# Low parts of the input projection's weights: from one GpSimd subtraction per block to two VectorE pieces

## The chip, the cores and the metric

The kernel runs on one core of one Trainium2 chip, as one program. The metric is device time in microseconds (us), the median of three runs. Engines are named as in the profile: PE is TensorE (PEld its weight loads), DVE is VectorE, ACT is ScalarE, POOL is GpSimd, SP is the engine from whose queue most DMAs are issued.

## What is computed

One decoder layer over 1024 tokens of width 1024, in float32: a combined input projection that feeds a sparse attention branch (NSA) and an RWKV-7 branch, their merge, a cross-attention, and a grouped mixture of experts. What matters here is the first step and its two users:

```python
z_nsa, z_rwkv, z_gate = split(x @ w_in)          # x: 1024 tokens by 1024
o_nsa  = nsa_attention(...)                      # reads z_nsa
o_rwkv = rwkv7_time_mix(...)                     # reads z_rwkv; a scan over the tokens
y = (sigmoid(..) * (o_nsa @ p_nsa) + sigmoid(..) * (o_rwkv @ p_rwkv)) @ w_out
```

The operands of the projection's matmuls are split in two: a high part (the value rounded to fp32r) and a low part (the value minus its high part). A product is then three matmuls: high by high, low by high, high by low.

## The kernel before, in words

The input projection goes by blocks of 128 output columns, 41 in all (40 of 128 columns and one of 24). For each block `weights` loads 512 KB of w_in into the tile `wraw` (one buffer, line 114, on SP's queue), rounds it into `wh` on ACT (line 117, one instruction of 128x1024) and subtracts to get `wl` on POOL (line 118, one instruction of 128x1024). `wh` and `wl` have two buffers each, so the weights of one block are made while the block before is multiplied. `halves` then runs, for each half of the tokens, 8 groups of three matmuls (lines 35 to 37: `xh,wh`, `xl,wh` and `xh,wl`; only the third reads `wl`) into one of two PSUM banks, and an evacuation on ACT or DVE or both: lines 220 to 227 for RWKV blocks, 184/185, 198/199 and 209 for attention blocks, 238 for the 16 gate blocks. The evacuated tile `ev` (three buffers) is stored to memory.

The first two blocks (12 and 13 of the RWKV columns) are made while x itself is loaded, transposed on PE (line 74) and split by ACT and DVE (line 28).

Beside the blocks run 8 items of the RWKV branch (`Rwkv.steps`). Each item forms its factors on ACT, DVE and POOL, inverts triangular matrices by rows on DVE (lines 850 and 851: 31 pairs of short instructions between SBUF tiles, `xinv` and `tinv`), applies the inverses on PE (line 869, evacuated at 872, 875, 877 and 880), and then runs a chain of 8 sequential steps on PE and ACT (lines 902, 904, 908, 909). The end of an item (lines 916 to 938) normalises its output. After the last item the RWKV buffers are given to the attention, whose loads and compression (`Nsa.__init__`, `compress`, lines 335 to 390) run beside the last gate blocks; then the attention proper begins on PE at lines 465 and 467.

The order of the blocks and items in the program is a string written out by hand (`ORDER`). The order of instructions on each engine's queue is not: the framework's context (`schedule_with_timeline_sim=True` in `kernel`) lays every queue out before the run, by its own estimate of when each instruction could begin. So projection matmuls stand between the small matmuls of the RWKV items one by one. On the chip each queue runs strictly in the order laid out: an instruction that has to wait holds up all that stand behind it on its engine.

Of the kernel before, what the change touches and what calls it, by code (L numbers as in the profile page):

```python
# [7 lines left out]
F32 = mybir.dt.float32  # L8
# [3 lines left out]
ALU = mybir.AluOpType  # L12
# [69 lines left out]
class Inproj:  # L82
# [28 lines left out]
    def weights(self, c0, w, p0=None):  # L111
        nc, pw = self.k.nc, self.pw
        raw = (p0.tile([128, 8, 128], F32, tag="wraw0", bufs=2, name="wraw0") if p0 else pw.tile([128, 8, 128], F32, tag="wraw", bufs=1, name="wraw"))[:, :, :w]
        nc.sync.dma_start(raw, self.w_in[:, :, c0:c0 + w])
        wh = pw.tile([128, 8, 128], F32R, tag="wh", bufs=2, name="wh")[:, :, :w]
        wl = pw.tile([128, 8, 128], F32R, tag="wl", bufs=2, name="wl")[:, :, :w]
        nc.scalar.copy(wh, raw)  # L117
        nc.gpsimd.tensor_tensor(wl, raw, wh.bitcast(F32), ALU.subtract)  # L118
        return wh, wl

    def ev(self, dt=F32):
# [91 lines left out]
    def r_block(self, b, weights=None, tag=None):  # L213
        nc, s = self.k.nc, self.k.s
        st = {}

        def evac(acc, ns):
            t, o = self.ev(), self.ev()
            m, m1 = self.mu[:, b:b + 1], self.mu1[:, b:b + 1]
            nc.scalar.mul(t, acc, m)  # L220
            nc.vector.scalar_tensor_tensor(o[:, 1:], acc[:, 1:], m1, t[:, :511], ALU.mult, ALU.add)
            if ns.start == 0:
                nc.vector.tensor_scalar(o[:, :1], acc[:, :1], m1, None, ALU.mult)
                st["c"] = self.pw.tile([128, 1], F32, tag="rc", bufs=2, name="rc")
                nc.gpsimd.tensor_scalar(st["c"], t[:, 511:512], 1.0, 1.0, ALU.mult, ALU.mult)
            else:
                nc.vector.scalar_tensor_tensor(o[:, :1], acc[:, :1], m1, st["c"], ALU.mult, ALU.add)
            nc.sync.dma_start(s["r", b][:, ns], o)
        if weights:
            return self.halves(*weights, evac, tag)  # L230
        self.block(1304 + 128 * b, evac)
# [162 lines left out]
class Nsa:  # L394
# [47 lines left out]
    def attention(self):  # L442
# [6 lines left out]
        with tc.tile_pool(name="nq", reuse_waits="tile", bufs=1) as self.pq, tc.tile_pool(name="nw", reuse_waits="tile", bufs=2) as pw, tc.tile_pool(name="np", reuse_waits="tile", bufs=2, space=PSUM) as ps:  # L449
            def front(br, g, qt, t, st):  # L450
# [6 lines left out]
                for i in range(4):  # L457
# [18 lines left out]
                    st[br, i] = pt  # L476
                    yield
                w = weights(g, qt, sums, slice(bi + 1, bi + 2))
                for i in range(4):
                    nc.gpsimd.tensor_scalar(st[br, i][:, :n], st[br, i][:, :n], w[:, 0, i:i + 1], 1.0, ALU.mult, ALU.mult)  # L480
# [11 lines left out]
            def compressed(g, qt, t, st):  # L492

                qs = slice(128 * qt, 128 * qt + 128)
                sums = pw.tile([128, 1, 4], F32, tag="csum", name="csum")
                sc = ps.tile([128, 512], F32, tag="pt", bufs=PTB, name="sc")
                for i in range(4):
                    o = sc[:, 64 * i:64 * i + 64]
                    nc.tensor.matmul(o, t["q"][:, i, qs], kch[:, g, :], start=True, stop=False)
                    nc.tensor.matmul(o, t["q"][:, i, qs], kcl[:, g, :], start=False, stop=True)  # L500
                pc = pw.tile([128, 4, 64], F32, tag="pc", name="pc")
                mc = pw.tile([128, 4], F32, tag="mc", name="mc")
                nc.vector.tensor_tensor(pc, sc[:, :256].rearrange("p (h n) -> p h n", h=4),
                                        tcm[:, 4 * g:4 * g + 4, 56 - 8 * qt:120 - 8 * qt], ALU.add)
                nc.vector.tensor_reduce(mc, pc, AX.X, ALU.max)
                nc.vector.tensor_scalar(mc, mc, -1e29, None, ALU.max)
                nc.gpsimd.tensor_tensor(pc, pc, mc.unsqueeze(2).to_broadcast([128, 4, 64]), ALU.subtract)
                nc.scalar.activation(pc, pc, AF.Exp)
                nc.vector.tensor_reduce(sums[:, 0], pc, AX.X, ALU.add)
                w = weights(g, qt, sums, slice(0, 1))  # L510
                nc.gpsimd.tensor_tensor(pc, pc, w[:, 0, :].unsqueeze(2).to_broadcast([128, 4, 64]), ALU.mult)
                st["c"] = pc
# [1405 lines left out]
```

## Time and profile before

| what | value |
| --- | --- |
| median of 3 runs | 1859.53 us (1857.18 to 1862.02) |
| the profiled execution's own time | 1859.28 us |
| its span on the core | 1857.5 us |
| mean granted TensorE clock | 0.961 of full |

The span is what the trace covers; the time of an execution has 1.8 us more around it. Rows of the trace give a start and a duration in us from the span's start; in a timeline row a bracket at the end gives how long the engine stood idle before the instruction and what released it.

### The profile page before, as it was taken

What the parts mean: (1) busy time and instruction counts of PE and PEld (TensorE: products, weight loads), DVE (VectorE), ACT (ScalarE), POOL (GpSimd) and SP (SyncE); (2) the same over time, 40 slices, a digit from 0 to 9 for tenths busy, and PEclk for the clock granted to TensorE, in tenths of its full rate; (3) what the DMA queues carried; (4) which work ended last, traced back from release to release, by engine and by line L of the source; (5) the groups of instructions that cost most, each with busy time, mean ns of one, the idle gap of its engine ahead of it and who ended that gap; (6) DMA issues with size and microseconds to landing.
All of it is one profiled execution on the core that took longest, in us unless ns stands there. A gap on an engine that the chain in (4) does not pass through costs nothing. (4 is left out here: it accounts for less than half of the span.)

```text
span 1857.5 us, 27257 instructions
## 1 busy us (share of the span) xinstructions
PE 1740.5 (94%) x9254; PEld 1419.5 (76%) x9254; DVE 1203.8 (65%) x2738; ACT 845.1 (45%) x1756; POOL 534.5 (29%) x681
## 2 busy tenths in 40 slices
PE   8999989999999999999998899999997999999992
PEld 6877767787678878888886678877796888888871
DVE  3225757768775202599886675556986777777786
ACT  4223313344333221398886441034304676676672
POOL 1123202222122211266566121100024333333214
PEclk9999979999999999999999899999978999999996
DMA  7354335344523228702102764033324999999974
GB/s 230 117 177 119 114 112 166 114 139 128 147 84 89 93 81 245 239 10 83 41 10 64 245 196 161 23 99 125 135 93 149 317 294 296 294 300 303 310 278 151
DMA packets 252797, 295.95 MB, mean 159 GB/s; under 512 B 63789, under 2 KB 150981, under 8 KB 252144
## 3 DMA queue, kind: packets, MB, share of 16 engines
q1 hardware_dynamic: 245184, 273.52, 45.1%
q0 software_dynamic: 7472, 20.67, 4.6%
q8 instruction: 74, 1.21, 0.3%
q14 instruction: 67, 0.55, 0.1%
HBM read 231.88 MB, written 70.98 MB: 163 GB/s over the span
## 5 line engine op out<-in xcount | busy, mean ns | idle before, releaser
L35 PE MATMUL acc<-xh,wh 128*128 128x512 f32 (+1 forms) x656 | 268.1, 409 | 8.4 <-ACT wh L117 3.3
L36 PE MATMUL acc<-xl,wh 128*128 128x512 f32 (+1 forms) x656 | 268.6, 410 | 0.0
L37 PE MATMUL acc<-xh,wl 128*128 128x512 f32 (+1 forms) x656 | 266.6, 407 | 0.2 <-POOL wl L118 0.2
L1529 DVE TENSOR_TENSOR wlo<-wraw,whi 128x512 fp32r<-128x512 f32 x384 | 237.6, 684 | 32.3 <-ACT whi L1528 32.0
L1528 ACT CAST whi<-wraw 128x512 fp32r<-128x512 f32 x384 | 206.1, 621 | 19.3 <-issue 17.8
L118 POOL TENSOR_TENSOR wl<-wraw,wh 128x1024 fp32r<-128x1024 f32 (+1 forms) x41 | 99.0, 2414 | 295.0 <-ACT wh L117 284.5
L35 PEld LDWEIGHTS acc<-xh,wh 128*128 128x128 f32 (+1 forms) x656 | 124.2, 189 | 44.1 <-ACT wh L117 4.2
L37 PEld LDWEIGHTS acc<-xh,wl 128*128 128x128 f32 (+1 forms) x656 | 123.9, 189 | 36.0 <-issue 8.1
L36 PEld LDWEIGHTS acc<-xl,wh 128*128 128x128 f32 (+1 forms) x656 | 124.4, 190 | 33.9 <-issue 6.6
L475 ACT ACTIVATE pp<-pp,nm 128x640 f32<-128x640 f32 (+7 forms) x128 | 94.1, 737 | 8.2 <-DVE nm L474 7.7
L28 DVE TENSOR_TENSOR pl<-ptp,ph 128x512 fp32r<-128x512 f32 x132 | 87.4, 684 | 10.6 <-ACT ph L28 10.0
L35 PE MATMUL eacc<-whi,exh 128*128 128x512 f32 x240 | 94.0, 392 | 0.0
L36 PE MATMUL eacc<-wlo,exh 128*128 128x512 f32 x240 | 93.9, 391 | 0.0
L37 PE MATMUL eacc<-whi,exl 128*128 128x512 f32 x240 | 93.7, 391 | 0.0
L1637 POOL DMA_INDIRECT accd<-ey,ef x32 | 54.5, 1705 | 124.5 <-ACT whi L1528 53.6
L480 POOL TENSOR_SCALAR pp<-pp,wgt 128x640 f32<-128x640 f32 (+7 forms) x128 | 88.0, 711 | 0.6
L908 ACT COPY state<-rseq 64x64 f32<-64x64 f32 x128 | 26.6, 208 | 125.3 <-PE rseq L904 99.5
L979 POOL TENSOR_SCALAR lnrs<-lnmv 128x1 f32<-128x1 f32 x21 | 18.0, 858 | 225.9 <-DVE lnmv L978 206.9
L117 ACT CAST wh<-wraw 128x1024 fp32r<-128x1024 f32 (+1 forms) x41 | 42.3, 1031 | 87.2 <-PE acc L36 43.1
L850 DVE TENSOR_TENSOR tinv<-xinv,ln 128x60 f32<-128x60 f32 (+24 forms) x248 | 66.9, 270 | 23.0 <-DMA ln<-ld 16.6
L28 ACT CAST ph<-ptp 128x512 fp32r<-128x512 f32 x132 | 73.7, 581 | 16.6 <-PE ptp L534 15.6
L534 PE MATMUL ptp<-ident,pp 128*128 128x128 f32 x528 | 79.8, 276 | 0.7 <-DVE pl L28 0.5
(497 smaller groups left out, 4393.1 us busy)
## 6 DMA issues: line engine op xcount, KB each, us to landing
wraw<-in_moe_w_up SPq DMA_DIRECT2D x32, 1024.0 KB
wraw<-in_moe_w_gate SPq DMA_DIRECT2D x32, 1024.0 KB
wraw<-in_moe_w_down SPq DMA_DIRECT2D x32, 1024.0 KB
wraw<-in_w_in SPq DMA_DIRECT2D x40, 512.0 KB
sm<-ev SPq DMA_DIRECT2D x32, 256.0 KB
sr<-ev SPq DMA_DIRECT2D x28, 256.0 KB
skew<-skew SPq DMA_DIRECT2D x1, 4608.0 KB
xraw<-in_x SPq DMA_DIRECT2D x8, 512.0 KB
```

The costliest lines, as they stand in the source:

```text
L28: x = nc.scalar.copy(hi, src), (nc.gpsimd if by_pool else nc.vector).tensor_tensor(lo, src, hi.bitcast(F32), ALU.subtract)
L35: nc.tensor.matmul(out, ah, bh, start=start, stop=False)
L36: nc.tensor.matmul(out, ah, bl, start=False, stop=False)
L37: nc.tensor.matmul(out, al, bh, start=False, stop=stop)
L118: nc.gpsimd.tensor_tensor(wl, raw, wh.bitcast(F32), ALU.subtract)
L475: nc.scalar.activation(pt[:, :n], pt[:, :n], AF.Exp, bias=nm, scale=-1.0, accum_out=sums[:, 0, i:i + 1])
L480: nc.gpsimd.tensor_scalar(st[br, i][:, :n], st[br, i][:, :n], w[:, 0, i:i + 1], 1.0, ALU.mult, ALU.mult)
L534: nc.tensor.transpose(tp[:, 128 * i:128 * i + 128], st[br, i][:, c0:c0 + 128], ident)
L850: nc.vector.tensor_tensor(tmp[:, :m, :w], x[:, :m, j:j + 1].to_broadcast([128, m, w]), ln[:, j:j + 1, j + 1:].to_broadcast([128, m, w]), A ...
L1528: nc.scalar.copy(hi[:, cs], raw[:, cs])
L1529: (nc.gpsimd if i in LOPOOL else nc.vector).tensor_tensor(lo[:, cs], raw[:, cs], hi[:, cs].bitcast(F32), ALU.subtract)
L1637: nc.gpsimd.indirect_dma_start(out=self.acc, out_offset=bass.IndirectOffsetOnAxis(ap=ix, axis=0), in_=y[r, :], in_offset=None, compute_op= ...
```

## The change

`weights` forms `wl` with two VectorE instructions of 128x512 each (of 128x96 each in the block of 24 columns) and uses no GpSimd instruction. Nothing else is edited: the cast of line 117 stays one ScalarE instruction, buffers, DMAs and the hand-written order stay. The queues of all engines are laid out anew for the changed program.

```diff
         nc.scalar.copy(wh, raw)
-        nc.gpsimd.tensor_tensor(wl, raw, wh.bitcast(F32), ALU.subtract)
+        for i in range(2):
+            cs = slice(4 * i, 4 * i + 4)
+            nc.vector.tensor_tensor(wl[:, cs], raw[:, cs], wh[:, cs].bitcast(F32), ALU.subtract)
         return wh, wl
```

## Rows read from the trace of the kernel before

**Rows 1.** The page's first line.

```profile
span 1857.5 us, 27257 instructions
```

**Rows 2.** Busy time of each engine by stage; columns PE, PEld, DVE, ACT, POOL, PEclk.

```profile
184.00:600.00 416.00, 399.86 (x2490) 316.08 (x2489) 299.90 (x882) 153.30 (x337) 94.44 (x73) 0.96 0.41 121
0.00:184.00 184.00, 173.15 (x821) 138.16 (x822) 64.11 (x125) 58.35 (x92) 42.35 (x41) 0.98 0.53 162
600.00:775.00 175.00, 172.90 (x915) 143.03 (x914) 41.02 (x88) 42.00 (x101) 31.40 (x16) 1.00 0.53 164
```

**Rows 3.** The page's groups of instructions, lines 118 and 117.

```profile
L118 POOL TENSOR_TENSOR wl<-wraw,wh 128x1024 fp32r<-128x1024 f32 (+1 forms) x41 | 99.0, 2414 | 295.0 <-ACT wh L117 284.5
...
L117 ACT CAST wh<-wraw 128x1024 fp32r<-128x1024 f32 (+1 forms) x41 | 42.3, 1031 | 87.2 <-PE acc L36 43.1
```

**Rows 4.** Who waited for whom, 0 to 780 us: total us, times, longest.

```profile
SPq L114 <- POOL wl L118: 26.3, 18, 6.1
...
PE acc L37 <- POOL wl L118: 0.2, 1, 0.2
```

**Rows 5.** Timeline around the stage's end, SP's queue and PE.

```profile
707.82 1.29 SPq L435 DMA_DIRECT2D nq<-sq  x3
...
774.07 0.22 PE L465 MATMUL sp<-nk,nq 128*128 128x128 f32 x1
```

**Rows 6.** A VectorE group of the same form, and its timeline.

```profile
L1529 DVE TENSOR_TENSOR wlo<-wraw,whi 128x512 fp32r<-128x512 f32 x384 | 237.6, 684 | 32.3 <-ACT whi L1528 32.0
...
1804.48 1.28 DVE L1529 TENSOR_TENSOR wlo<-wraw,whi 128x512 fp32r<-128x512 f32 x2
```

**Rows 7.** One line's instructions, line 850: count, then ns min/median/max.

```profile
L850 DVE TENSOR_TENSOR tinv<-xinv,ln x248: 162/215/2445, 184.2 to 594.7; 128x60 f32<-128x60 f32 x12, 128x54 f32<-128x54 f32 x8, 128x66 f32<-128x66 f32 x8, 128x28 f32<-128x28 f32 x8
```

**Rows 8.** Timeline of DVE and POOL, long inversion steps: first, a middle one, last.

```profile
185.73 2.28 DVE L851 TENSOR_TENSOR xinv<-xinv,tinv 128x28 f32<-128x28 f32 x1
...
354.25 2.40 POOL L118 TENSOR_TENSOR wl<-wraw,wh 128x1024 fp32r<-128x1024 f32 x1 [4.19 <-ACT wh L117]
354.40 2.34 DVE L850 TENSOR_TENSOR tinv<-xinv,ln 128x68 f32<-128x68 f32 x1
...
584.17 2.05 DVE L851 TENSOR_TENSOR xinv<-xinv,tinv 128x70 f32<-128x70 f32 x1
```

**Rows 9.** Timeline of PE, four idle times ended by DVE.

```profile
243.16 0.80 PE L35 MATMUL acc<-xh,wh 128*128 128x512 f32 x1 [1.58 <-DVE ev L227]
...
360.23 0.41 PE L902 MATMUL rseq<-r_yv,r_f 128*128 128x64 f32 x2 [3.23 <-DVE r_yv L880]
...
430.34 1.12 PE L791 MATMUL rpa<-r_r,blk 128*128 128x512 f32 x2 [1.21 <-DVE r_r L789]
...
541.91 0.63 PE L927 MATMUL racc<-ident,r_ot 128*128 128x128 f32 x4 [1.49 <-DVE r_ot L924]
```

**Rows 10.** Stretches behind three of these; columns as in rows 2.

```profile
243.00:249.00 6.00, 5.84 (x14) 4.58 (x15) 4.22 (x19) 0.00 (x0) 0.00 (x0) 0.50 0.49 141
...
361.50:365.00 3.50, 3.50 (x11) 2.81 (x10) 2.93 (x13) 0.51 (x2) 0.00 (x0) 0.52 0.63 188
...
543.40:546.50 3.10, 3.10 (x8) 1.93 (x7) 3.10 (x7) 0.57 (x2) 0.00 (x0) 0.59 0.28 82
```

**Rows 11.** Timeline of PE behind the cast of the last block but one.

```profile
736.26 7.43 PE L364 MATMUL cacc<-cz,cw 128*128 128x126 f32 x64
743.44 0.48 PE L37 MATMUL acc<-xh,wl 128*128 128x512 f32 x1
```

**Rows 12.** Timeline of PE in the start.

```profile
12.61 0.66 PE L74 MATMUL tp<-ident,xraw 128*128 128x128 f32 x4 [0.23 <-DVE xl L28]
```

**Rows 13.** Instructions on the tile wl by stage; columns PE, PEld, POOL, PEclk.

```profile
184.00:600.00 416.00, 119.83 (x290) 54.58 (x290) 43.67 (x19) 0.96 0.41 121
```

**Rows 14.** Timeline of POOL, the longest wl but one.

```profile
144.85 2.87 POOL L118 TENSOR_TENSOR wl<-wraw,wh 128x1024 fp32r<-128x1024 f32 x1
```

**Rows 15.** What ACT waited for, 184 to 600 us.

```profile
ACT wh L117 <- PE acc L36: 24.4, 12, 6.1
```

## The prediction

> **What bounds the kernel now.** The page's first line [rows 1] and the table above give the account: 1857.5 us of span, 1859.28 us for that execution, so 1.8 us lie around the span; the sum below is made against 1859.28, which is 0.25 us under the median of the runs. Next read the busy time by stage [rows 2]. The projection fills the first 775 us. In all three of its stages PE is busy for 94 to 99% of the time, DVE for 35, 72 and 23%, POOL for 23, 23 and 18%. So PE's queue is the bound, and what counts is only PE's idle time and the time in which its granted clock is at the lower level. The reader is to see that neither engine that the edit touches is short of time as a whole, but that DVE is dense from 184 to 600 us, where the RWKV inversions are.
>
> The groups [rows 3] give the edited line: 41 subtractions of 2.41 us on POOL, each behind a cast of 1.03 us on ACT. The wait list [rows 4] says whether anybody misses the result: PE waited 0.2 us for `wl` in all. SP's queue waited 26.3 us in 18 pieces to reload `wraw`, which hides, since a reload has a whole block's time. So a shorter latency of `wl` is worth nothing by itself. The stage hands over without a gap: the RWKV buffers go to the attention's loads at 707.8 us, and PE reaches the first attention matmul at 774.07 us, straight behind the last projection matmul [rows 5]. Nothing later is tied to absolute time, so what PE gains or loses before 774 us I pass on unchanged.
>
> **What the edit takes from POOL.** 41 instructions of 2.41 us, 99 us of POOL time [rows 3]. POOL is no bound, so the time itself is worth nothing. What it does to DVE is. Inversion steps of lines 850 and 851 take 0.215 us in the median and up to 2.4 us [rows 7]; ten of the 496 take over 1.2 us beside a `wl`, the first at 185.73 us and the last at 584.17 us, 21.6 us together. Each of them lies over a `wl` of POOL and ends when it ends: at 354.25 us POOL starts for 2.40 us, at 354.40 us a step starts that lasts 2.34 us [rows 8]. So ten of the 19 `wl` of this stretch [rows 13] stop DVE, for 21.6 - 10 x 0.215 = 19.4 us.
>
> What stands behind on DVE's queue is late by that, and four times PE runs into it: 1.58, 3.23, 1.21 and 1.49 us of idle time ended by DVE [rows 9], 3 to 10 us behind the start of a blocked step (at 239.25, 354.40, 420.83 and 538.88 us; the second is the one shown [rows 8]). That is 7.5 us. Behind three of them PE's matmuls go at the 1.2 GHz level: granted 0.50 over 6.0 us, 0.52 over 3.5 us and 0.59 over 3.1 us [rows 10], a loss of 3.0 + 1.7 + 1.3 = 6.0 us. Together 13.5 us of PE time follow from 19.4 us of blocked DVE, 0.70 us per us.
>
> **What it puts on DVE.** 82 instructions. The nearest row is the same operation on the same shape between SBUF tiles in the expert stage: 684 ns, and 1.28 us for two in a row [rows 6]. A block costs DVE 1.28 us; the small block's two pieces are bounded by 0 and 1.28 us and taken as 0.4. From 184 to 600 us that is 18 x 1.28 + 0.4 = 23.4 us against 19.4 us no longer blocked: DVE stays at about 73%. Before 184 us (12 blocks) and after 600 us (10) DVE is idle for two thirds and more [rows 2], which hides it; without that cover it would be 15.4 and 12.8 us of DVE.
>
> **What comes of the four stalls.** Two bounds. If the queues kept their order, DVE would spend 1.28 us where it was blocked for 2.09, 2.13, 1.66 and 2.06 us, so each stall shrinks by 0.81, 0.85, 0.38 and 0.78 us: 2.8 us, and the clock might fall as before. If the new layout counts the pieces as DVE's work, all 13.5 us go. The layout does place other work where `wl` is not yet there: behind the cast of the last block but one it runs 7.4 us of compression matmuls before the first matmul that reads `wl` [rows 11]. The 3.23 us stall, by contrast, had projection matmuls ready behind it, so the layout had not foreseen the late DVE. I lean to the upper end and take 9 us of gain.
>
> **What can be lost.** The nine other blocks of the stretch stopped no inversion; there the pieces are new work, 11.5 us of DVE: 0 us if foreseen, 11.5 x 0.70 = 8.0 us if each hits PE as the blocks did. Being part of the layout, they are nearer to the first: 1 us. In the start the pieces of the second block fall among the splits of x, on which PE waited only 0.23 us at a time [rows 12]: 0 to 1.28 us, I take 0.5. Waits are moved, too: the pieces wait for the cast where POOL did, and what stands behind them on DVE are inversion steps and evacuations, for which PE waits in turn; this is the third rival. SP's reload now waits for DVE, 1.1 us sooner if DVE comes at once; up to a block's time late it still hides.
>
> **Sum.** -9 + 1 + 0.5 = -7.5 us: 1859.28 - 7.5 = **1851.8 us**.
>
> One rule speaks against part of this. One `wl` took 2.87 us where 2.41 is usual, while an instruction of DVE with two SBUF inputs had started before it [rows 14]. The Trainium skill (SBUF — State Buffer, "Who interferes with whom") says that such a DVE instruction and a GpSimd instruction that reads SBUF exclude each other, and whichever issues second is held for the whole of the first. By that rule the new pieces hold up POOL's RWKV steps in turn: these fill 94.4 - 43.7 = 50.7 us of the 416, 12% [rows 2, 13], so some 4.6 of 38 pieces meet one, 3.1 us of lateness on POOL at most, 2.2 us at 0.70, and the sum would be 1854.0 us. I leave it out of the sum, since PE's waits that end in POOL come to 0.2 us in this stage [rows 4].
>
> **Rivals.** *The stalls only move* (no change). DVE's work in the dense stretch is the same to 4 us, PE takes its operands from the same queue, and the laid-out order has no spare. The 0.70 us per us then holds for the net 4.0 us: +2.8 us, 1862.1 us. For it: PE also waited for DVE where no block was near. Against it: those waits are short, and the four above are the four longest that DVE ended in the stretch.
>
> *DVE parks behind the cast* (slower). The pieces wait on ACT's cast, which in this stretch waited 24.4 us in 12 pieces for PE to finish with the buffer [rows 15]. POOL could afford to stand there; on DVE's queue inversions and evacuations stand behind. Parked for these waits and 12 casts of 1.03 us, DVE loses 36.8 us, of which 72%, its busy share, displaces work: 26.5 us, at 0.70 it is 18.6 us of PE. With the other terms 1859.28 - 7.5 + 18.6 = 1870.4 us. It decides when more than (7.5 + 5.6) / 0.70 = 18.7 us of DVE work is displaced. Against it: where ACT waits for PE, DVE mostly waits for PE as well.
>
> *POOL's other instructions block just the same*, so that the edit does not free the inversions: then DVE only gains work, and it is the first rival's time.
>
> **How the numbers follow.** 0.3%, about what a measurement of this kernel can tell from no change, is 5.6 us. The forecast has a chance of 0.47, its own range going from all 13.5 us gained (1845.8) to 1854. The first rival with the third has 0.31, the parked DVE 0.22. The queues of the whole program are laid out anew, which can shift PE's idle time by a few us anywhere; for that I widen downwards to 1844. Upwards the range takes in both rivals to 1870, so that the far half of the parked case and a larger gain are left out, some 2 in 10. Faster 0.47, same 0.31, slower 0.22.
>
> **What would show it.** In the changed kernel's trace no step of lines 850 and 851 lasts over 1.2 us beside a `wl`; line 118's successor is 82 instructions on DVE of some 0.68 us; DVE's busy time from 184 to 600 us is within 5 us of 299.9; PE's idle time ended by DVE in that stretch falls by several us, with fewer spells at the 1.2 GHz level behind it; the first attention matmul comes 5 to 13 us before 774. I am wrong if DVE's waits for ACT's cast come to 18 us or more, or if PE's waits for DVE keep their sum under other names.

## The result and the profile after

The changed kernel takes 1845.11 us (median of 6 runs, 1839.17 to 1850.26) against 1861.08 us in the runs of before beside it: a ratio of 0.9919, 95% interval 0.9902 to 0.9936. By that ratio it is faster by some 15 us (the two medians lie 16.0 us apart), twice the 7.5 us that I forecast. The profiled execution took 1847.55 us; its page begins so, and has this group for the edited line:

```profile
span 1845.8 us, 27287 instructions
...
L120 DVE TENSOR_TENSOR wl<-wraw,wh 128x512 fp32r<-128x512 f32 (+1 forms) x82 | 52.3, 676 | 62.3 <-ACT wh L117 62.0
```

The 41 subtractions of 2.41 us on POOL [rows 3] are 82 of 0.68 us on DVE. The busy time by stage, same columns as in [rows 2]:

```profile
0.00:184.00 184.00, 176.41 (x852) 142.41 (x853) 82.17 (x171) 60.55 (x96) 14.13 (x29) 1.00 0.55 167
184.00:600.00 416.00, 402.24 (x2545) 322.37 (x2544) 297.84 (x905) 155.68 (x347) 49.47 (x53) 0.98 0.42 124
600.00:775.00 175.00, 169.46 (x899) 140.19 (x897) 56.21 (x151) 48.88 (x129) 14.48 (x29) 0.98 0.52 165
```

In the middle stage DVE took over 23.8 us of subtractions and is still busy for 297.84 us against 299.90: it gave up as much time held as it got in work. At 184 us PE is already 31 matmuls further (852 for 821), which I had not expected. The two lines of the inversion (850 and 851 before):

```profile
L852 DVE TENSOR_TENSOR tinv<-xinv,ln x248: 151/212/1117, 179.9 to 585.7; 128x60 f32<-128x60 f32 x12, 128x54 f32<-128x54 f32 x8, 128x66 f32<-128x66 f32 x8, 128x28 f32<-128x28 f32 x8
...
L853 DVE TENSOR_TENSOR xinv<-xinv,tinv x248: 160/214/634, 180.2 to 585.9; 128x60 f32<-128x60 f32 x12, 128x54 f32<-128x54 f32 x8, 128x66 f32<-128x66 f32 x8, 128x28 f32<-128x28 f32 x8
```

The longest step was 2.445 us [rows 7]. Counting all over 0.9 us, there were 12 of 23.8 us together; now there is one, of 1.12 us. What PE waited for from 184 to 600 us, and DVE's wait for the cast in that stretch (total us, times, longest):

```profile
PE rpa L742 <- DMA r_k<-z: 6.0, 1, 6.0
PE acc L35 <- DVE ev L28: 2.2, 1, 2.2
PE ntacc L290 <- DMA ev<-in_c_t: 2.2, 1, 2.2
PE rpa L766 <- DVE r_cs L762: 1.6, 1, 1.6
PE racc L871 <- DVE r_z L874: 1.4, 1, 1.4
...
DVE wl L120 <- ACT wh L117: 7.9, 2, 7.6
```

The four longest stalls that DVE ended were 7.5 us [rows 9]; now three of 5.2 us stand in their place. All of PE's idle time in the stretch that DVE ended comes to 11.3 us before and 5.3 us now. The part that a DMA ended went the other way, from 2.4 to 8.2 us, with the 6.0 us of the first line above as the largest piece. And the stage's end, on PE's timeline:

```profile
759.00 0.30 PE L467 MATMUL sp<-nk,nq 128*128 128x128 f32 x1 [1.36 <-DVE vc L392]
```

The attention begins 15.1 us sooner than at 774.07 [rows 5]. Up to there PE has the same matmuls (4212 before, 4213 after), so the 15.1 us must be idle time or a lower clock. I add both up by stage: the idle time is the stretch less PE's busy time; the loss at the 1.2 GHz level is (1 - granted clock) times the length, summed over windows of 4 us.

| stage | before: idle + clock loss | after | difference |
| --- | --- | --- | --- |
| start, 0 to 184 us | 10.9 + 3.4 = 14.3 | 7.6 + 0.0 = 7.6 | -6.7 |
| stretch, 184 to 600 us | 16.1 + 15.4 = 31.5 | 13.8 + 10.2 = 24.0 | -7.5 |
| end, 600 us to the attention | 2.1 + 0.0 = 2.1 | 4.3 + 0.0 = 4.3 | +2.2 |

Of the stretch's 7.5 us, 2.3 are idle time and 5.2 are clock: the new waits for DMAs take back nearly all of the idle time that DVE no longer ends. The sum of the three stages is 12.0 us; the other 3.1 us lie in PE's busy time and I can put them to no row. Behind the attention's start 3.4 us are given back in this execution (spans 1857.5 and 1845.8 us, 11.7 apart).

**The start.** In the kernel before, PE stood for a late cast at 136 us, and its clock fell behind it. SP's queue, ACT, PE and the window (columns as in [rows 2]) there:

```profile
113.06 0.43 SPq L644 DMA_DIRECT2D rmask<-in_c_rmask  x1
...
128.99 0.38 SPq L114 DMA_DIRECT2D wraw<-in_w_in  x1
...
135.23 1.04 ACT L117 CAST wh<-wraw 128x1024 fp32r<-128x1024 f32 x1 [2.74 <-DMA wraw<-in_w_in]
...
136.32 0.80 PE L35 MATMUL acc<-xh,wh 128*128 128x512 f32 x1 [2.66 <-ACT wh L117]
```

```profile
135.00:145.00 10.00, 8.68 (x21) 5.38 (x22) 5.89 (x8) 6.11 (x9) 6.89 (x7) 0.66 0.49 161
```

The same in the changed kernel:

```profile
111.68 0.38 SPq L114 DMA_DIRECT2D wraw<-in_w_in  x1
112.11 0.58 SPq L646 DMA_DIRECT2D rmask<-in_c_rmask  x1
...
120.43 1.05 ACT L117 CAST wh<-wraw 128x1024 fp32r<-128x1024 f32 x1 [4.63 <-PE acc L36]
```

```profile
135.00:145.00 10.00, 10.00 (x41) 7.27 (x40) 6.69 (x12) 5.30 (x9) 4.33 (x6) 1.00 0.56 164
```

The low part of the block at 110 us is ready at 111.6 us (113.6 before), and the new layout puts the reload of `wraw` ahead of the RWKV branch's loads on SP's queue, where it had stood behind them. One more block's weights are ready when PE waits for that branch's data, and the wait and the spell at 1.2 GHz are gone. I had written that SP's reload hides; at this one place it didn't.

### The profile page after: what moved, and what is told of

Its sections match the earlier page's. It is cut to its first block, busy times and chain, and to the rows that moved or that the text cites. A ratio compares the mean times of both kernels' runs of the same rounds, so it can differ in the third digit from the quotient of the medians.

```text
span 1845.8 us, 27287 instructions
## 1 busy us (share of the span) xinstructions
PE 1725.1 (93%) x9254; PEld 1410.5 (76%) x9254; DVE 1226.0 (66%) x2820; ACT 844.1 (46%) x1756; POOL 436.9 (24%) x640
## 5 line engine op out<-in xcount | busy, mean ns | idle before, releaser
L36 PE MATMUL acc<-xl,wh 128*128 128x512 f32 (+1 forms) x656 | 264.5, 404 | 0.0
L120 DVE TENSOR_TENSOR wl<-wraw,wh 128x512 fp32r<-128x512 f32 (+1 forms) x82 | 52.3, 676 | 62.3 <-ACT wh L117 62.0
L28 ACT CAST ph<-ptp 128x512 fp32r<-128x512 f32 x132 | 73.8, 582 | 16.8 <-PE ptp L536 15.8
L852 DVE TENSOR_TENSOR tinv<-xinv,ln 128x60 f32<-128x60 f32 (+24 forms) x248 | 54.2, 218 | 34.3 <-DMA ln<-ld 28.5
L536 PEld LDWEIGHTS ptp<-ident,pp 128*128 128x128 f32 x528 | 64.4, 141 | 15.1 <-DVE pl L28 2.9
L467 PE MATMUL sp<-nk,nq 128*128 128x320 f32 (+5 forms) x192 | 71.5, 376 | 3.4 <-DVE nm L476 1.7
```

The lines of the kernel that those rows point to most:

```text
L28: x = nc.scalar.copy(hi, src), (nc.gpsimd if by_pool else nc.vector).tensor_tensor(lo, src, hi.bitcast(F32), ALU.subtract)
L36: nc.tensor.matmul(out, ah, bl, start=False, stop=False)
L467: nc.tensor.matmul(sp[:, o], t["q"][:, i, qs], t["k", br, "h"][:, kk], start=True, stop=False)
L536: nc.tensor.transpose(tp[:, 128 * i:128 * i + 128], st[br, i][:, c0:c0 + 128], ident)
L852: nc.vector.tensor_tensor(tmp[:, :m, :w], x[:, :m, j:j + 1].to_broadcast([128, m, w]), ln[:, j:j + 1, j + 1:].to_broadcast([128, m, w]), A ...
```

## The experiments

The theory: GpSimd's instruction, since it reads SBUF, holds up DVE's inversion steps, and PE pays for their lateness. Rivals: it is DVE's load that counts; the gain lies in the smaller pieces; or it lies in the start. Diffs are against the changed kernel unless said otherwise. Every kernel's queues are laid out anew. The table gives, for all, the sums defined above and the inversion steps over 0.9 us:

| kernel | ratio to before, interval | start | stretch | both | end | long steps, us |
| --- | --- | --- | --- | --- | --- | --- |
| before | | 14.3 | 31.5 | 45.8 | 2.1 | 12, 23.8 |
| the change | 0.9919 (0.9902 to 0.9936) | 7.6 | 24.0 | 31.6 | 4.3 | 1, 1.1 |
| e1 one piece | 0.9882 (0.9860 to 0.9905) | 7.8 | 20.2 | 28.0 | 4.2 | 2, 2.1 |
| e2 GpSimd, two pieces | 0.9950 (0.9932 to 0.9968) | 7.8 | 38.2 | 46.0 | 3.9 | 18, 22.1 |
| e3 GpSimd reads again | 1.0124 (1.0101 to 1.0147) | 15.5 | 37.3 | 52.8 | 16.3 | 16, 25.9 |
| e4 GpSimd writes only | 0.9943 (0.9924 to 0.9961) | 10.6 | 20.0 | 30.6 | 7.2 | 3, 3.2 |
| e5 more VectorE work | 0.9993 (0.9978 to 1.0009) | 7.9 | 29.3 | 37.2 | 12.3 | 2, 2.0 |
| e6 19 blocks on VectorE | 0.9877 (0.9854 to 0.9901) | 13.4 | 14.4 | 27.8 | 2.6 | 1, 1.1 |
| e7 22 others on VectorE | 0.9978 (0.9962 to 0.9995) | 7.8 | 34.1 | 41.9 | 3.6 | 14, 24.9 |
| e8 four pieces | 0.9910 (0.9885 to 0.9934) | 8.1 | 27.9 | 36.0 | 4.2 | 3, 3.3 |
| e9 as e6, one piece | 0.9891 (0.9874 to 0.9909) | 13.8 | 15.8 | 29.6 | 4.9 | 1, 1.1 |
| e10 as e6, others in two pieces | 0.9947 (0.9926 to 0.9967) | 7.4 | 26.8 | 34.2 | 5.6 | 0 |
| e11 before, start in two pieces | 0.9983 (0.9968 to 0.9997) | 7.2 | 45.1 | 52.3 | 2.7 | 11, 21.4 |

PE's idle time in the stretch that DVE ended sorts the kernels in the same way. It is 8.6 to 12.8 us in the four with GpSimd's low part in the blocks beside the inversions and nothing added (before, e2, e7, e11), and 2.4 to 5.4 us in the six with VectorE's (the change, e1, e6, e8, e9, e10). A single pair of kernels proves little, since each has its own layout: e2, with 18 long steps, and e10, with none, have the same time within the noise (0.9950 and 0.9947). The sums come from one execution of each kernel; e2's lies 7.2 us and e11's 5.9 us above its median, e7's 4.3 us below.

**Is it the pieces, or the engine?** e1 uses one VectorE instruction for the block, e8 four (`range(4)`, slices of two), e2 keeps two pieces but on GpSimd:

```diff
-            nc.vector.tensor_tensor(wl[:, cs], raw[:, cs], wh[:, cs].bitcast(F32), ALU.subtract)
+            nc.gpsimd.tensor_tensor(wl[:, cs], raw[:, cs], wh[:, cs].bitcast(F32), ALU.subtract)
```

> The low part on VectorE in one instruction of 128x1024 per block. Theory (GpSimd's subtraction stopped the inversion steps, and PE ran into what came late behind them): GpSimd is as free of it as in the change, so the time is the change's, 1841 to 1850 us, and no inversion step lasts over 1.2 us beside a low part. Rival (the two pieces matter, since a longer instruction holds up VectorE's queue): 1850 us or more, with PE's idle time ended by VectorE up by 3 us or more between 184 and 600 us. Rival (chance of the layout: any re-laid program lands somewhere within 10 us): anywhere from 1838 to 1862 us, with no relation to blocked steps.

> The low part on GpSimd as before, but in two instructions of 128x512. Theory: GpSimd reads the same amount, so inversion steps are stopped again, in pieces of about 1.2 us, some ten to twenty of them with 10 to 20 us in all; 1855 to 1863 us. Rival (two pieces are what helps, whatever the engine): 1841 to 1850 us. Rival (chance of the layout): anywhere from 1838 to 1862 us, whatever the blocked steps come to.

> VectorE in four pieces of 128x256 per block. One piece gave 1839.9 us, two 1845.1 us. If an instruction's fixed part is what tells them apart (two of 512 take 1.28 us against 1.22 us for one of 1024; four of 256 at 0.33 us apart take some 1.4 us), the time goes on rising: 1847 to 1855 us. If the difference is the layout's scatter, anywhere from 1838 to 1850 us. No long inversion steps in either case.

Measured: 1839.9 us for one piece (1.1 us below the theory's range), 1843.92 for four. With 1845.11 us for two pieces that is no trend, and the intervals of the three ratios overlap. The number of pieces on VectorE is worth nothing that can be told from a new layout. On GpSimd two pieces take 1852.4 us, which is in neither range, 2.6 us below the theory's and 2.4 us above the rival's. Timeline of POOL and DVE in that kernel:

```profile
228.49 0.19 DVE L853 TENSOR_TENSOR xinv<-xinv,tinv 128x29 f32<-128x29 f32 x1
228.60 2.50 POOL L120 TENSOR_TENSOR wl<-wraw,wh 128x512 fp32r<-128x512 f32 x2 [8.62 <-ACT wh L117]
228.71 1.20 DVE L852 TENSOR_TENSOR tinv<-xinv,ln 128x28 f32<-128x28 f32 x1
229.95 1.20 DVE L853 TENSOR_TENSOR xinv<-xinv,tinv 128x28 f32<-128x28 f32 x1
```

Each piece holds one step to the piece's end, so two steps in a row are held for about as long together as one was before. Start and stretch together are as before (46.0 and 45.8). The profiled execution (1859.58 us) lies 7.2 us above the median, and the half per cent that the median gains shows in no stage of it; that is left open.

**Is it the reading?** Both kernels add GpSimd work behind the change's pieces, into `wraw`, whose content nobody reads any more: e3 one more subtraction, e4 three fills that read nothing.

```diff
             nc.vector.tensor_tensor(wl[:, cs], raw[:, cs], wh[:, cs].bitcast(F32), ALU.subtract)
+        nc.gpsimd.tensor_tensor(raw, raw, wh.bitcast(F32), ALU.subtract)
```

```diff
             nc.vector.tensor_tensor(wl[:, cs], raw[:, cs], wh[:, cs].bitcast(F32), ALU.subtract)
+        for i in range(3):
+            nc.gpsimd.memset(raw, 0.0)
```

> The change, plus one GpSimd subtraction of 128x1024 per block from the same tiles whose result (written over wraw, after VectorE's pieces) nobody reads. The low part still comes from VectorE. Theory: the blocked inversion steps come back, about ten of 1.2 us and more with some 20 us in all between 184 and 600 us, on top of VectorE's own pieces; 1855 to 1867 us. Rival (the gain is that the low part comes 1.1 us sooner, or that VectorE makes it): the low part is as early as in the change, so 1841 to 1850 us. Rival (chance of the layout): anywhere from 1838 to 1862 us.

> As the run before it, but the extra GpSimd work is three fills of wraw, some 2.8 us per block, which write and read nothing. Theory (it is GpSimd's reading through what VectorE's two-input steps need, not GpSimd being busy): no inversion step over 1.2 us beside the fills, 1841 to 1850 us. Rival (GpSimd being busy holds up the RWKV steps on its own queue, and that was the price before): 1853 us or more without long inversion steps.

Measured: 1884.56 us for e3, 17.6 us past the theory's upper end, and 1850.32 us for e4, 0.3 us past the theory's upper end: 34 us between them. Timeline of e3:

```profile
264.89 2.39 POOL L121 TENSOR_TENSOR wraw<-wraw,wh 128x1024 f32<-128x1024 f32 x1 [28.90 <-DVE xinv L854]
265.01 0.41 DVE L896 TENSOR_TENSOR r_gp<-racc,r_gp 128x256 f32<-128x256 f32 x1
265.34 1.98 DVE L853 TENSOR_TENSOR tinv<-xinv,ln 128x24 f32<-128x24 f32 x1
...
320.24 2.39 POOL L121 TENSOR_TENSOR wraw<-wraw,wh 128x1024 f32<-128x1024 f32 x1
320.31 2.87 DVE L927 TENSOR_TENSOR r_ot<-r_ot,var 128x512 f32<-128x512 f32 x1
```

The second pair is no inversion step: an instruction of 128x512 with both inputs in SBUF, 0.68 us in the median, is held as well. The table's long steps are thus not all that is held. Timeline of e4, and its inversion line (min/median/max ns):

```profile
312.20 2.97 POOL L122 MEMSET wraw<- 128x1024 f32 x3 [9.18 <-DVE wl L120]
312.74 0.21 DVE L854 TENSOR_TENSOR tinv<-xinv,ln 128x48 f32<-128x48 f32 x1
312.98 0.21 DVE L855 TENSOR_TENSOR xinv<-xinv,tinv 128x48 f32<-128x48 f32 x1
313.22 0.21 DVE L854 TENSOR_TENSOR tinv<-xinv,ln 128x49 f32<-128x49 f32 x1
```

```profile
L854 DVE TENSOR_TENSOR tinv<-xinv,ln x248: 158/214/1117, 180.4 to 582.9; 128x60 f32<-128x60 f32 x12, 128x54 f32<-128x54 f32 x8, 128x66 f32<-128x66 f32 x8, 128x28 f32<-128x28 f32 x8
```

From 184 to 600 us, 45 inversion steps start beside a fill; their median is 0.21 us and the longest takes 0.57 us, though POOL is busy there for 100.88 us, more than in the kernel before. e4's three long steps stand beside GpSimd's RWKV instructions. So neither POOL's load nor its place in the order is what holds the steps, but that it reads. Both kernels also keep `wraw` longer. What ACT and PE waited for up to 780 us in e3, and ACT's wait in e4:

```profile
ACT wh L117 <- DMA wraw<-in_w_in: 35.8, 9, 8.8
...
PE acc L35 <- ACT wh L117: 4.8, 1, 4.8
```

```profile
ACT wh L117 <- DMA wraw<-in_w_in: 35.5, 12, 7.7
```

In e4 this costs PE 4.5 us, so it does not tell the two apart; it may be what makes e4 slower than the change. The 34 us are not all the holding's: of the 40.3 us between the two profiled executions 10.0 lie behind the first attention matmul, where neither kernel has such work, and no row explains them.

**Is it DVE's load?** e5 gives DVE two more subtractions of 128x1024 per block, again into `wraw`:

```diff
+        for i in range(2):
+            nc.vector.tensor_tensor(raw, raw, wh.bitcast(F32), ALU.subtract)
```

> The change, plus two more VectorE subtractions of 128x1024 per block (written over wraw, read by nobody): some 2.4 us more of VectorE per block, 45 us more between 184 and 600 us, twice what the blocked steps took before, but laid out as VectorE's own work. Theory (what cost time was lateness that the layout had not counted, not VectorE's load): the 45 us cost far less than 0.70 us each, 1845 to 1858 us. Rival (VectorE's time is what counts, 0.70 us of PE per us whatever its kind): 1845 + 0.70 x 45 = 1877 us.

```profile
184.00:600.00 416.00, 395.21 (x2412) 313.53 (x2410) 326.33 (x880) 148.41 (x321) 51.66 (x51) 0.98 0.41 123
```

DVE is busy for 28.5 us more in the stretch than with the change, and the time is 1858.38 us, 13 us more: 0.4 us past the theory's upper end, and far from the rival's 1877. The stretch does not hold the same work here, since the inversions end later, at 630 us for 586 with the change:

```profile
L855 DVE TENSOR_TENSOR xinv<-xinv,tinv x248: 116/216/1049, 193.7 to 630.0; 128x60 f32<-128x60 f32 x12, 128x54 f32<-128x54 f32 x8, 128x66 f32<-128x66 f32 x8, 128x28 f32<-128x28 f32 x8
```

So all three stages must be read together. Their sum is 49.5 us for 35.9 with the change: 13.6 us more, 8.0 of them in the end. Even if all of it is laid to the 40 added subtractions that start in the stretch (some 48 us of DVE), that is 0.28 us of PE per us. The kernel before lost 12.0 us more than the change by the same three sums, for 19.4 us held: 0.62. In e3, where DVE's busy time rose by 19.6 us (to 317.46 us), nearly all of it holding, the three sums rose by 33.2 us, PE's waits for `wraw` among them. So a microsecond of held DVE costs PE at least twice what a microsecond of added work does. That the layout leaves room for the work, which it knows, and none for the holding, which it doesn't, fits this; no trace shows the layout's own estimates, so it is argued and not shown.

**Where is the gain?** e6 uses VectorE only in the 19 blocks beside the inversions, e7 only in the other 22 (12 in the start, 10 at the end); e9 is e6 with one piece. The diff of e6; e7 negates the condition:

```diff
+        self.nw = getattr(self, "nw", -1) + 1
+        if 12 <= self.nw < 31:
             for i in range(2):
...
+        else:
+            nc.gpsimd.tensor_tensor(wl, raw, wh.bitcast(F32), ALU.subtract)
```

> VectorE's two pieces only in the 19 blocks whose weights are made beside the inversions (the 13th to the 31st); GpSimd in the 22 others. Theory (the gain comes from the inversion steps alone): nearly all of the gain, 1843 to 1851 us, no long inversion steps. Rival (the gain comes from the start or from the stage's end, where GpSimd also stops VectorE): 1853 us or more.

> The converse: VectorE's two pieces in the 22 other blocks, GpSimd in the 19 beside the inversions. Theory: as before the change, 1857 to 1864 us, with ten or so long inversion steps of 15 to 22 us in all. Rival (start or end of the stage): 1850 us or less. Rival (chance of the layout): this run and the one with the 19 blocks come out in no relation to long steps.

> VectorE forms the low part in one piece of 128x1024, and only in the 19 blocks beside the inversions; GpSimd forms the others. If one piece and 19 blocks were each a gain of their own (1839.9 us with one piece in all blocks, 1836.4 us with two pieces in 19), the two add to 1830 to 1835 us, ratio 0.985 or below. If what lies between those kernels is only the scatter of newly planned layouts, as I believe, this one lies anywhere in 1834 to 1848 us, ratio 0.986 to 0.993. By both, no long step of the inversions stands beside a low part in 184 to 600 us.

Measured: e6 1836.44 us, the fastest of all and 6.6 us below the theory's range; e7 1854.36 us, 2.6 us below its range, with 14 long steps of 24.9 us where I expected ten or so of 15 to 22; e9 1840.68 us. The inversion line in e6, then in e7:

```profile
L856 DVE TENSOR_TENSOR tinv<-xinv,ln x248: 166/215/1117, 183.6 to 583.1; 128x60 f32<-128x60 f32 x12, 128x54 f32<-128x54 f32 x8, 128x66 f32<-128x66 f32 x8, 128x28 f32<-128x28 f32 x8
```

```profile
L856 DVE TENSOR_TENSOR tinv<-xinv,ln x248: 127/216/2332, 180.0 to 593.3; 128x60 f32<-128x60 f32 x12, 128x54 f32<-128x54 f32 x8, 128x66 f32<-128x66 f32 x8, 128x28 f32<-128x28 f32 x8
```

Nearly all of the gain sits in the 19 blocks (0.9877 for e6, 0.9978 for e7). e9 fell where scatter puts it, above the sum of two gains. But e6 keeps the start's stall (13.4 us) and has the smallest stretch (14.4 us), while the change has a small start and 24.0 us in the stretch. Do the two trade against each other? e10 is e6 with GpSimd in two pieces in the other blocks; e11 is the kernel before with two pieces in its first 12 blocks alone, both on GpSimd. Diff of e11, against before:

```diff
-        nc.gpsimd.tensor_tensor(wl, raw, wh.bitcast(F32), ALU.subtract)
+        self.nw = getattr(self, "nw", -1) + 1
+        for i in range(2 if self.nw < 12 else 1):
+            cs = slice(4 * i, 4 * i + 4) if self.nw < 12 else slice(0, 8)
+            nc.gpsimd.tensor_tensor(wl[:, cs], raw[:, cs], wh[:, cs].bitcast(F32), ALU.subtract)
```

> VectorE forms the low part in two pieces in the 19 blocks beside the inversions; in the other 22 blocks GpSimd does, in two pieces of 128x512 in place of one of 128x1024. Until 184 us, PE's idle time and loss at 1.2 GHz came to 14.3 us before and 13.4 us with the 19 blocks alone, both with a wait of 2.7 us for a late cast at 136 us, and to 7.6 to 8.1 us in the kernels with two or more pieces, or VectorE, in the start, where the reload of wraw stands ahead of the RWKV loads on SP's queue (111 to 113 us, 129 us otherwise). Theory A, the two gains add: the start falls from 13.4 to 8 us and the stretch from 184 to 600 us stays at 14 to 16 us, so 1836.4 - 5.5 = 1831 us (1828 to 1834). Theory B, what PE gains in the start is projection work that is then missing beside the inversions: the start falls to 8 us, the stretch rises to 18 to 24 us, and the time is 1836 to 1845 us.

> The kernel before, with GpSimd's subtraction in two pieces in the first 12 blocks alone. The wait for the cast at 136 us goes, and the start's idle time and loss at 1.2 GHz fall from 14.3 to 8 us. GpSimd still holds the inversions, with some ten long steps of up to 2.4 us. Theory A: those 6 us are kept, 1860 - 6 = 1854 us, ratio 0.996 to 0.998, and the stretch from 184 to 600 us stays at 31 to 32 us. Theory B: most is given back beside the inversions, which rise to 34 to 38 us, 1857 to 1862 us.

Measured: 1850.19 and 1857.43 us. In both the reload comes at 112.9 us, and the start falls to 7.4 and 7.2 us; in both the stretch grows by more than that, to 26.8 us (14.4 in e6) and 45.1 us (31.5 before). Busy time by stage in e10; then the longest of PE's waits in it, the next projection matmul on PE's queue, and the cast of the next block:

```profile
0.00:184.00 184.00, 176.57 (x852) 142.72 (x853) 68.82 (x135) 60.42 (x95) 46.40 (x53) 1.00 0.54 167
184.00:600.00 416.00, 401.13 (x2541) 319.98 (x2540) 299.58 (x914) 155.85 (x350) 51.35 (x53) 0.97 0.42 123
```

```profile
281.76 2.08 PE L877 MATMUL racc<-r_rr,dt 128*128 128x128 f32 x8 [8.13 <-DMA dt<-xd]
...
285.76 0.79 PE L37 MATMUL acc<-xh,wl 128*128 128x512 f32 x1
...
287.45 1.04 ACT L117 CAST wh<-wraw 128x1024 fp32r<-128x1024 f32 x1 [0.89 <-PE acc L36]
```

What B says of the sums holds in its direction, and beyond its ranges: e10 is 5 us above its time, and both stretches are above theirs (18 to 24 us and 34 to 38 us). e11's median lies in B's range, but its sums are those of an execution 5.9 us above that, so their size says little. The other kernels fit: those with the early reload and nothing added lose 20.2 to 27.9 us in the stretch with VectorE there and 34.1 to 45.1 us with GpSimd, those with the late reload 14.4 and 15.8 us (e6, e9) and 31.5 us (before).

B's reason is argued and not shown: the projection matmuls that PE does sooner in the start, of which there is a fixed number, would be missing beside the inversions. Where PE waits 8.1 us for a load in e10, little projection work was ready: the last four matmuls of a block, which stand behind the waiting one on PE's queue, and no weights of the next block, whose cast comes at 287.45 us. That the early start is what left it so, no run shows; 531 projection matmuls are still to come at 600 us. The start by itself is worth 0.2% (e11; 0.3% at the interval's end) and comes with a loss of 0.7% in company of the 19 blocks (e10 against e6; there GpSimd's last ten blocks are in two pieces as well).

## Why the prediction was right, and where it was off

**The cause** held. PE's queue is the bound; GpSimd's subtraction stopped the inversions; the stalls and the spells at 1.2 GHz behind them were the price. Of the long steps one is left, and GpSimd's reading is what makes them (e3, e4). PE's idle time ended by DVE in the stretch fell by 6.0 us, as I said. The first attention matmul moved the way I said, though by 15.1 us where I gave 5 to 13.

**The costs on DVE** held: 0.68 us a piece, 23.8 us in the stretch for 23.4 forecast, DVE's busy time within 2.1 us of 299.9. "1 us" for the nine other blocks can't be taken apart from the rest.

**The size.** The step that failed is "I lean to the upper end and take 9 us of gain". Since work moves between start and stretch, the two must be read together. The four kernels with GpSimd in the 19 blocks have 41.9 to 52.3 us there, 46.5 in the mean; the six with VectorE 27.8 to 36.0, 31.2 in the mean. That is 15.3 us, and for the change itself 14.2 us: the whole of my upper bound of 13.5 us and a little more. The mean ratios of the two groups (0.9978 and 0.9904) say nearly the same, 0.74% or 13.7 us, from all executions. I had shown 0.70 us of PE time per us held and then charged only two thirds of it; 14.2 / 19.4 is 0.73. The other terms of the sum, 1.5 us of loss, can't be seen in these sums. The 1845.11 us lie below 1845.8, where the whole of my upper bound is gained; my range holds them only through the widening to 1844 for the new layout, so that the number lies in it is in part luck.

**The start** I put at 0.5 us of loss, and the reload at nothing. It was 6.7 us of gain there, by a reload 17 us sooner. In the change this stands in place of a larger gain in the stretch: 7.5 us, about the 8 us net that I forecast for it, but e6 and e9, whose start is as before, get 17.1 and 15.7 us. That the stretch came out near its number was thus partly luck and no proof of the sum.

**The rivals.** The stalls did not only move, but idle time did in part: PE's waits for DVE fell from 11.3 to 5.3 us in the stretch, and its waits for DMAs rose by 5.8 us. What is gained there is mostly clock. DVE did not park: it waited 62.0 us for the cast over the whole stage, but 7.9 us in the stretch, in 2 pieces, against the 18.7 us of displaced work from which that rival decides. GpSimd's other instructions do block inversion steps as well, only for shorter. With the change nine steps last 0.5 to 1.12 us beside a GpSimd instruction of the RWKV branch, 5.7 us together; before there were 13, of 8.8 us, besides the ten at the low part. That the edit frees nothing is refuted all the same. The longest:

```profile
297.46 1.04 POOL L885 TENSOR_TENSOR r_gp<-i,ec 128x512 f32<-128x512 f32 x1
297.47 1.12 DVE L852 TENSOR_TENSOR tinv<-xinv,ln 128x69 f32<-128x69 f32 x1
```

That DVE's new pieces hold up GpSimd in turn, which the 1854.0 us were for, shows no cost: none of PE's waits in the stretch is ended by POOL.

**After the stage** I assumed nothing changes. From the first attention matmul to the end of the span, the changed kernel needed 1086.8 us for 1083.4 before; the other kernels but e3 need 1077 to 1086 us, so a few us of the medians' differences lie there and have no cause that I can name.

## What to carry to other kernels

When a short instruction of one engine lasts as long as an instruction of another beside it, add up the time so held and look for what waits behind it; here some three quarters of it reached the bound engine (14.2 of 19.4 us), and moving the holder's work to the held engine cost less than it gave, although that was the denser one. Moving the work only where it holds something up was enough: e6 (1836.44 us) was the best version run, though with one piece the 19 blocks alone (e9, 1840.68 us) did no better than all 41 (e1, 1839.9 us). And before a stall is counted as a gain, ask what work PE would do in its place: when it is work that would fill a later gap, the gain may only be moved, as the sums of start and stretch suggest here.

## What the runs showed of the hardware

What is held goes by operands. The ten inversion steps of the kernel before that started beside GpSimd's subtraction, with both inputs in SBUF, lasted until it ended, but instructions with one input in PSUM ran at their own length (0.42 us in the median of each of the two below). Timeline of e7 (`rtp` is in PSUM):

```profile
209.56 2.39 POOL L124 TENSOR_TENSOR wl<-wraw,wh 128x1024 fp32r<-128x1024 f32 x1 [4.33 <-ACT wh L117]
209.66 0.41 DVE L815 TENSOR_TENSOR r_lo<-rtp,rmask 128x256 f32<-128x256 f32 x1
209.99 0.42 DVE L816 TENSOR_TENSOR r_f<-rtp,rmask 128x256 f32<-128x256 f32 x1
```

I had not expected copies between SBUF tiles to be held as well. Timeline of e2:

```profile
328.82 3.01 POOL L120 TENSOR_TENSOR wl<-wraw,wh 128x512 fp32r<-128x512 f32 x2 [12.28 <-PE acc L37]
...
330.58 1.27 DVE L777 COPY r_ar<-r_kkn 128x8 f32<-128x8 f32 x1
```

The same copy takes 0.17 us in e4, with no GpSimd instruction beside it:

```profile
368.14 0.17 DVE L779 COPY r_ar<-r_kkn 128x8 f32<-128x8 f32 x1
```

The Trainium skill (SBUF — State Buffer, "Who interferes with whom") says that a VectorE instruction contends with GpSimd when it has two SBUF inputs and GpSimd reads SBUF, or when it is a copy or a scalar operation in one of its two-port modes, and that a GpSimd instruction that only writes does not disturb the former. The inversion steps, the rows of e7 and the 45 steps beside the fills of e4 agree with the first and the last of these. The copy of e2 was held too, but no row shows in which mode it ran.
